# A decoder layer in split precision: three of four output pieces split by adding transfers, output pieces first in a block

## The chip, the cores and the metric

The kernel runs on one core of one Trainium2 chip. The core has a matrix engine (TensorE, here PE, whose weight loads the profile lists as PEld), a vector engine (VectorE, DVE), an activation engine (ScalarE, ACT), a general engine (GpSimd, POOL) and a queue engine (SyncE, SP). Transfers are issued from the queues of SP, ACT and POOL and carried by 16 DMA engines. SBUF is the on-chip memory, PSUM the small memory into which PE accumulates. The metric is device time in microseconds (us), lower is better.

## The reference

One decoder layer on 256 tokens of width 2048, in float32: a half-step SwiGLU FFN, layer norm, a mixer with sparse attention and a gated recurrence, layer norm, a second half-step FFN, layer norm. The change touches only the two FFNs. Of the reference, cut:

```
def swiglu(h, w_in, w_out):
    a, b = jnp.split(h @ w_in, 2, axis=-1)
    return (jax.nn.silu(a) * b) @ w_out
...
    h = layer_norm(DN_ALPHA * h + 0.5 * swiglu(h, ffn1_w_in[l], ffn1_w_out[l]), ln1_g[l], ln1_b[l])
    ... # mixer
    h = layer_norm(DN_ALPHA * h + 0.5 * swiglu(h, ffn2_w_in[l], ffn2_w_out[l]), ln3_g[l], ln3_b[l])
```

The inner width is 5632, so `w_in` is 2048 x 11264 and `w_out` 5632 x 2048.

## The kernel before

**Split precision.** PE multiplies in a format (fp32r) narrower than float32. Every operand is split into a high part (rounded by an ACT copy) and a low part (what is left), and a product is three matmuls: high x high, high x low, low x high (lines 743 to 745). The weights are used once each, so all of them have to be split while the kernel runs. That is the work of class `Weights`.

**Pieces.** All weights, in the order of their use, form one list of pieces. PE takes them one by one (`unit`, L282). A piece is one of these:

- An *output piece* ("o" in a plan): 128 x 1024 of `w_out`, 12 matmuls of 512 columns. It is loaded into a `raw` tile (4 buffers).
- A *form*: the `w_in` weights of a block come as four chunks, 1 MB each, in `rf` tiles (two buffers and a third that is used every third time). A chunk is multiplied by a scheme with seven products in place of eight, in four forms that need sums of sub-blocks: `p1q3` (12 matmuls of 256 columns; its sum `ws`, L230), `p2` (6; its sum is written at L234), `q5p7` (12; L237 writes a sum that q4p6 will need, and q5p7 reads `ws`), `q4p6` (12).

**Two ways to split.** The usual way (`split_to`, L246): ACT copies the piece to the high part of an `hl` tile (L275), DVE subtracts to get the low part (L276). There are five `hl` buffers. The other way, for pieces in the list `far` (`far_to`, L167): ACT writes minus the rounded value into two half-width tiles `wd` (L182), a POOL transfer then *adds* the weights from memory into them (L183), which leaves the low part, and ACT copies the high part into two more `wd` tiles (L185). Such a piece uses ACT and the transfers and no DVE. Its four `wd` tiles come from the pool of 128 x 512 tiles with tag `u`, which has 53 buffers and also holds the activations (`xs` or `hs`, 16 tiles), their sums for the forms (`sh`, `sl`, 16 tiles) and the gated activations `g`.

**The order.** The instructions of PE, SP and POOL run in program order; those of ACT and DVE are ordered by the framework's scheduler. When PE comes to piece `cur`, `unit` first splits far pieces up to `cur + 12` (EARLY) and loads far pieces up to 4 (LOADS) beyond those, then loads other pieces up to `cur + 8`, splits them up to `cur + 4` (AHEAD), and then takes one step of the background tasks.

**Blocks and segments.** An FFN has 22 blocks of 256 inner columns, in segments (`SEGS`) of 2 and then five times 4 blocks. For each block PE computes the products of `w_in`; DVE and ACT apply the gate (`gate`, tile `z`, L1132 to L1145). Some pieces into the next block PE transposes the result (L1151), and ACT and DVE split it into two `g` tiles (L878, L879). How many pieces after the block this happens is LAG_T, (7, 6): 7, and 6 for the last block. A segment of four blocks makes eight `g` tiles. They are multiplied by `w_out` during the *next* segment: each of its four blocks takes one quarter nb of the output columns, in four output pieces k = 0, 2, 4, 6, piece k using `g[k]` and `g[k+1]`. The product is then copied (`yd`, L1174) and added to memory by a POOL transfer (L1175).

The plan of a block says where its output pieces stand among its 16 forms. In blocks 6 to 21 three stand at the front and one behind the eighth form (`block_plan` with `lead` 3). Far pieces are those with k = 2 and 6; in the first segment's outputs, which have k = 0 and 2 only, k = 2 of the last two quarters.

Of the kernel before, what the change touches and what calls it, by code (L numbers as in the profile page):

```python
# [22 lines left out]
SEGS = ((0, 2), (2, 6), (6, 10), (10, 14), (14, 18), (18, 22))  # L23
# [39 lines left out]
AHEAD = 4  # L63
EARLY = 12
LOADS = 4
FORMS = ("p1q3", "p2", "q5p7", "q4p6")
PIECE = 1024
FAST = (0, 1, 2, 3)
# [4 lines left out]
def block_plan(chunks, fills, lead=2, n=4, late=True):  # L73

    plain = [("c", k) for q in range(n) if q not in chunks for k in (4 * q, 4 * q + 2)]
    forms = [(f, q) for q in chunks for f in FORMS]
    rest = ["o"] * fills
    plan = [(rest.pop(), 0) for _ in range(min(lead, fills))] + plain[:1]  # L80
    plain = plain[1:]
    slow = []
    while plain or rest:
        for which in (plain, rest) if late else (rest, plain):
            if which:
                p = which.pop(0)
                slow.append((p, 0) if p == "o" else p)
    if not forms:
        return plan + slow
    step = len(forms) / (len(slow) + 1)  # L90
    n = 0
    for i, f in enumerate(forms):
        plan.append(f)
        while len(slow) > n and i + 1 >= (n + 1) * step:
            plan.append(slow[n])
            n += 1
    return plan


FOUR = tuple(range(6, 22))  # L100


def layer_plans():
    three = (1, 2, 3)
    plans = [block_plan((), 0)] * 2
    plans += [block_plan((1, 3), 2, 0)] + [block_plan(three, 2, 2, late=False)] * 3
    for n in range(6, NBK):
        plans.append(block_plan(FAST if n in FOUR else three, 4, 3))
    return plans


FILLS = [(g, nb, 2 * p) for g, (b0, b1) in enumerate(SEGS[:-1]) for nb in range(4) for p in range(b1 - b0)]
PLANS = layer_plans()
FAST_MORE = (2, 3, 1)
AWAY = (0, 1, 4, 7, 10, 13)
# [13 lines left out]
OUT_LAST = ([(nb, k) for nb in (0, 1) for k in (0, 2, 4)] + [(nb, 6) for nb in (0, 1)]  # L129
            + [(nb, k) for nb in (2, 3) for k in (0, 2, 4, 6)])  # L130

LAG_T = (7, 6)
LAG_LN = 4
WIDE = 2
LAG_ROPE = 6
# [2 lines left out]
class Weights:  # L138
# [28 lines left out]
    def far_to(self, i):  # L167


        nc = self.nc  # L170
        while self.far_loaded < len(self.far) and self.far[self.far_loaded] <= i + LOADS:
            k = self.far[self.far_loaded]
            ap = self.pieces[k][0]
            t = self.far_raw[k] = self.pool.tile([P, PIECE], F32, name=f"raw{k}", tag="raw", bufs=RAW_BUFS)
            nc.sync.dma_start(t, ap)
            self.far_loaded += 1
        while self.far_split < len(self.far) and self.far[self.far_split] <= i:
            k = self.far[self.far_split]
            ap, t = self.pieces[k][0], self.far_raw.pop(k)
            h, l = ([self.wide() for _ in range(2)] for _ in range(2))  # L180
            for c in range(2):
                nc.scalar.activation(l[c], t[:, c * 512:(c + 1) * 512], AF.Copy, scale=-1.0)  # L182
                nc.gpsimd.dma_start(l[c], ap[:, c * 512:(c + 1) * 512], accum_op=OP.add)  # L183
            for c in range(2):
                nc.scalar.activation(h[c], t[:, c * 512:(c + 1) * 512], AF.Copy)  # L185
            self.hl[k] = (h, l)
            self.far_split += 1
# [58 lines left out]
    def split_to(self, i, step=PIECE):  # L246
        nc = self.nc
        while self.split <= min(i, len(self.pieces) - 1):
# [28 lines left out]
            self.hl[self.split] = (h, l)  # L277
            if form in (None, FORMS[-1]):
                del self.raw[k]
            self.split += 1  # L280

    def unit(self, n):  # L282
        if self.cur < 0 or self.off == self.size(self.cur):
# [3 lines left out]
            self.far_to(self.cur + EARLY)  # L287
            self.load_to(self.cur + AHEAD + LOADS)
            self.split_to(self.limit or min(self.cur + AHEAD, self.cap))
# [78 lines left out]
def tile_layer(ctx, tc, x_fm, x_tm, pos, f1a, f1o, wA, wki, wB, wG, lru, wab, wrb, wo, f2a, f2o,  # L368
# [41 lines left out]
    def plain(aps):  # L410
        for ap in aps:
            for o in range(0, ap.shape[1], PIECE):
                pieces.append((ap[:, o:min(ap.shape[1], o + PIECE)], None))

    def block_pieces(ap, plan, fills=None, fo=None):
        chunk = {}
        for f, k in plan:
            if f == "c":
                pieces.append((ap[:, k * 512:k * 512 + PIECE], None))
            elif f == "o" and not fo:  # L420
                plain([next(fills)])
            elif f == "o":
                g, nb, k = next(fills)
                if k in (2, 6) and (g or nb >= 2):
                    far.append(len(pieces))
                k += 2 * SEGS[g][0]
                pieces.append((fo[nb][:, k * 512:k * 512 + PIECE], None))
            else:
                if k not in chunk:
                    chunk[k] = ap[:, k * 2048:(k + 1) * 2048]  # L430
                pieces.append((chunk[k], f))

    def ffn_pieces(fa, fo):
        fills = iter(FILLS)
        for n, plan in enumerate(PLANS):
            block_pieces(fa[n], plan, fills, fo)
        for nb, k in OUT_LAST:
            k += 2 * SEGS[-1][0]
            plain([fo[nb][:, k * 512:k * 512 + PIECE]])
# [5 lines left out]
    for i, b in enumerate(A_ORDER):  # L445
        if b is None:
            plain([wki])
        elif i == 0:
            plain([wA[b]])
        else:  # L450
            block_pieces(wA[b], PLANS_A[i], early)
    for b in range(6):
        block_pieces(wG[b], block_plan(GATE_FAST[b], 0, 0))
# [8 lines left out]
    for i in range(NR + LAG):  # L462
# [4 lines left out]
        if i >= LAG:  # L467
            g, c = divmod(i - LAG, TPG)
# [655 lines left out]
    def ffn(x, forms, ln):  # L1124
        def gate(c, e, g, i, lag, plain):

            z = W.fast_pool.tile([P, 4 * S], F32, name=name("z"), tag="z", bufs=Z_BUFS)
            z4 = z.rearrange("p (j c) -> p j c", j=4)
            a, b = z4[:, 0:4:2], z4[:, 1:4:2]
            if e:  # L1130
                p1, p6, p7, q5 = e[0][:, :S], e[0][:, S:], e[1][:, :S], e[1][:, S:]
                A.activation(z4[:, 0], p1, AF.Copy)  # L1132
                V.tensor_tensor(z4[:, 1], z4[:, 0], p6, op=OP.add)
                V.tensor_tensor(z4[:, 2], z4[:, 1], p7, op=OP.add)
                V.tensor_tensor(b, q5[:, None, :].to_broadcast([P, 2, S]), z4[:, 1:3], op=OP.subtract)
                for t in range(2):
                    w = 512 if plain or t == 0 else S
                    zt = z[:, t * 512:t * 512 + w]
                    V.tensor_tensor(zt, zt, c[t][:, :w], op=OP.add)  # L1139
                A.activation(a, a, AF.Silu)  # L1140
            else:
                for t in range(2):
                    A.activation(z4[:, 2 * t], c[t][:, :S], AF.Silu)
                    A.activation(z4[:, 2 * t + 1], c[t][:, S:], AF.Copy)
            V.tensor_tensor(a, a, b, op=OP.mult)  # L1145
            for _ in range(lag):
                yield
            ps = BP()
            for k in range(2):
                for t in range(2):  # L1150
                    T.transpose(ps[:, k * S + t * P:k * S + (t + 1) * P], z[:, t * 512 + k * P:t * 512 + (k + 1) * P], ident)  # L1151
            with tc.high_priority() if lag == LAG_T[1] else nullcontext():
                for k in range(2):
                    hl = UHL("g")
                    split(hl, ps[:, k * S:(k + 1) * S])
                    g[i + k] = hl
# [20 lines left out]
        for s, (b0, b1) in enumerate(SEGS):  # L1177
            for n in range(b0, b1):
                c, e = blockF(x, forms, PLANS[n], fill)
                task = gate(c, e, g[s], 2 * (n - b0), LAG_T[n == NBK - 1], ("c", 0) in PLANS[n])  # L1180
                with tc.high_priority():
# [268 lines left out]
    def product(x, forms, fast):  # L1450

        c, e = blockF(x, forms, block_plan(fast, 0, 0, len(x) // 4), None)
        return (joined(c, e), True) if e else (c, False)
# [9 lines left out]
    def fetch(src):  # L1463
        r = []
        for t in range(2):
            u = U("gf")
            G.dma_start(u, src[t])
            r.append(u)
        return r
# [10 lines left out]
    for nb in range(4):  # L1480
        g, got = got, fetch(ga[nb + 1]) if nb < 3 else None
        s, _ = product(ya, ya_forms, YA_FAST[nb])
# [43 lines left out]
    for j in range(-1, NR + LAG):  # L1526
# [15 lines left out]
        if j >= LAG:  # L1542
            i = j - LAG
            g, c = divmod(i, TPG)
# [48 lines left out]
    for nb in range(4):  # L1593
        if nb == 2:
            bg.add("main", residual(ln1_g, ln1_b, away))
        s, _ = product(yrs, yr_forms, YR_FAST[nb])
        g, a = got
# [98 lines left out]
```

## Time and profile before

| | us |
|---|---|
| median of 3 runs | 2341.34 (2337.8 to 2342.86) |
| the profiled execution | 2340.27 |
| its span, first to last instruction | 2338.4 |
| first FFN, blocks 6 to 21 | 502.31 |
| second FFN, blocks 6 to 21 | 502.11 |

The page of the profile gives the busy time of each engine as a share of the span. The table of windows gives the same for a stretch of the span, in the order PE, PEld, DVE, ACT, POOL, with the granted TensorE clock (1.00 is full), the mean busy share of the 16 DMA engines and the bandwidth. In a timeline each line has the start in us from the span's start, the duration in us, engine, line of the kernel, operation, the tile written and those read, and shapes. The duration of an instruction includes some overlap with the next one, so costs are read from start to start. "x2" marks two like instructions in a row. A bracket gives the idle time before an instruction and what ended it. In the list of waits stand the total in us, the number of waits, and the longest.

### The profile page before, as it was taken

Reading aid. Unit: us, or ns where it says so; the run is one execution under the profiler, and the core shown is the slowest. Engines: PE = TensorE matmul, PEld = TensorE weight load, DVE = VectorE, ACT = ScalarE, POOL = GpSimd, SP = SyncE. Lnnn points to the kernel's source line nnn. Section 1 sums busy time; section 2 is a strip of 40 time slices with the busy share of each in tenths; the row PEclk is TensorE's granted clock in tenths of the full one; section 3 lists DMA queues with packets and bytes.
Section 4 is the critical chain, followed back from the end, with each engine's and each line's share of the span. In section 5 each row is a group of like instructions: output and inputs, shape, how many; then the busy total and the mean of one; then the engine's idle time right before and its main releaser. Section 6 shows DMA issues by size and latency. Waiting matters only on the chain.

```text
span 2338.4 us, 40427 instructions
## 1 busy us (share of the span) xinstructions
PE 2312.5 (99%) x15430; PEld 2109.4 (90%) x15430; DVE 2201.5 (94%) x3196; ACT 1560.0 (67%) x2273; POOL 263.4 (11%) x368
## 2 busy tenths in 40 slices
PE   9999999999999999999999999999999999999998
PEld 7899999999988999888899998888889999999997
DVE  7999999999999999979887888998999999999997
ACT  7667777777757656556557785555667777777763
POOL 1101111111110000000100001100111111111111
PEclk9999999999999999999999999999999999999999
DMA  9878988888876556554675658655788888888875
GB/s 336 251 238 240 261 250 251 250 256 250 230 244 209 192 187 216 185 189 154 244 239 193 200 182 326 239 198 195 242 275 232 253 255 252 243 252 267 244 221 215
DMA packets 142178, 546.97 MB, mean 234 GB/s; under 512 B 16640, under 2 KB 17280, under 8 KB 117536
## 3 DMA queue, kind: packets, MB, share of 16 engines
q1 hardware_dynamic: 100800, 455.00, 55.1%
q0 software_dynamic: 41040, 89.27, 18.4%
q8 instruction: 120, 1.97, 0.3%
q14 instruction: 74, 0.61, 0.1%
q10 hardware_dynamic: 144, 0.13, 0.0%
HBM read 507.10 MB, written 37.22 MB: 233 GB/s over the span
## 4 chain that ended last, share of the span: by engine, by line
PE 66%; DVE 23%; issue 5%; DMA 3%; ACT 2%; POOL 0%; SPq 0%; ACTq 0%; DVEq 0%; POOLq 0%
PE mm L743 13%; PE mm L745 13%; PE mm L744 13%; DVE hl L276 13%; PE bp L744 5%; PE bp L745 5%; PE bp L743 4%; PE mm L1390 3%; PE mm L1389 3%; PE mm L1391 3%; DVE ws L230 2%; DVE rf L237 2%; DVE rf L234 2%; ACT hl L275 2%; DMA raw<-f1o 1%
## 5 line engine op out<-in xcount | busy, mean ns | idle before, releaser
L275 ACT ACTIVATE hl<-rf 128x1024 fp32r<-128x1024 f32 x573 | 511.3, 912 | 232.9 <-DVE rf L237 119.7
L276 DVE TENSOR_TENSOR hl<-rf,hl 128x1024 fp32r<-128x1024 f32 x573 | 596.9, 1047 | 8.2 <-ACT hl L275 3.8
L276 DVE TENSOR_TENSOR hl<-raw,hl 128x1024 fp32r<-128x1024 f32 (+3 forms) x402 | 474.2, 1196 | 62.2 <-ACT hl L275 61.4
L275 ACT ACTIVATE hl<-raw 128x1024 fp32r<-128x1024 f32 (+3 forms) x402 | 408.4, 1035 | 179.4 <-PE mm L745 82.8
L744 PE MATMUL bp<-hl,sh 128*128 128x256 f32 x1146 | 323.6, 282 | 10.1 <-DVE hl L276 10.1
L743 PE MATMUL bp<-hl,sh 128*128 128x256 f32 x1146 | 320.9, 280 | 0.0
L745 PE MATMUL bp<-hl,sl 128*128 128x256 f32 x1146 | 320.2, 279 | 0.0
L743 PE MATMUL mm<-hl,hs 128*128 128x512 f32 (+1 forms) x800 | 274.5, 343 | 1.6 <-DVE z L1139 0.7
L275 ACT ACTIVATE hl<-ws 128x1024 fp32r<-128x1024 f32 x191 | 202.0, 1058 | 102.7 <-DVE ws L230 71.5
L744 PE MATMUL mm<-hl,hs 128*128 128x512 f32 (+1 forms) x800 | 268.3, 335 | 0.0
L745 PE MATMUL mm<-hl,hs 128*128 128x512 f32 (+1 forms) x800 | 267.9, 335 | 0.1
L230 DVE TENSOR_TENSOR ws<-rf 128x1024 f32<-128x1024 f32 x191 | 233.8, 1224 | 5.4 <-DMA rf<-wrb 1.3
L276 DVE TENSOR_TENSOR hl<-ws,hl 128x1024 fp32r<-128x1024 f32 x191 | 234.2, 1226 | 1.8 <-ACT hl L275 1.7
L744 PEld LDWEIGHTS bp<-hl,sh 128*128 128x128 f32 x1146 | 215.4, 188 | 17.5 <-DVE hl L276 16.3
L745 PEld LDWEIGHTS bp<-hl,sl 128*128 128x128 f32 x1146 | 217.7, 190 | 0.0
L743 PEld LDWEIGHTS bp<-hl,sh 128*128 128x128 f32 x1146 | 215.4, 188 | 1.3
L1389 PE MATMUL mm<-hs,hl 128*128 128x256 f32 x640 | 178.3, 279 | 0.0
L1391 PE MATMUL mm<-hs,hl 128*128 128x256 f32 x640 | 177.8, 278 | 0.0
L1390 PE MATMUL mm<-hs,hl 128*128 128x256 f32 x640 | 177.7, 278 | 0.0
L743 PEld LDWEIGHTS mm<-hl,hs 128*128 128x128 f32 x800 | 150.4, 188 | 19.1 <-issue 2.6
L745 PEld LDWEIGHTS mm<-hl,hs 128*128 128x128 f32 x800 | 151.0, 189 | 16.7 <-DVE hs L937 0.5
L744 PEld LDWEIGHTS mm<-hl,hs 128*128 128x128 f32 x800 | 150.5, 188 | 14.3 <-DVE hl L276 0.2
(360 smaller groups left out, 5897.6 us busy)
## 6 DMA issues: line engine op xcount, KB each, us to landing
rf<-f1a SPq DMA_DIRECT2D x75, 1024.0 KB, 7.7
rf<-f2a SPq DMA_DIRECT2D x75, 1024.0 KB, 7.5
raw<-f1o SPq DMA_DIRECT2D x88, 512.0 KB, 6.6
raw<-f2o SPq DMA_DIRECT2D x88, 512.0 KB, 6.6
raw<-wB SPq DMA_DIRECT2D x80, 512.0 KB, 4.8
raw<-wG SPq DMA_DIRECT2D x54, 512.0 KB, 4.2
ya<-yd POOLq DMA_DIRECT2D x80, 256.0 KB, 7.4
rf<-wA SPq DMA_DIRECT2D x20, 1024.0 KB, 5.5
```

Source lines behind the costliest of these rows:

```text
L230: v.tensor_tensor(t, b[:, 0:4:3], b[:, 1:2].to_broadcast([P, 2, 2, 256]), op=OP.add)
L234: v.tensor_tensor(b[:, 1], t[:, 1], b[:, 0], op=OP.add)
L237: v.tensor_tensor(b[:, 0], b[:, 1], b[:, 2], op=OP.add)
L275: nc.scalar.activation(hp, src, AF.Copy)
L276: self.last = nc.vector.tensor_tensor(lp, src, hp, op=OP.subtract)
L743: T.matmul(ps, xh, w[0], start=start, stop=False)
L744: T.matmul(ps, xh, w[1], start=False, stop=False)
L745: T.matmul(ps, xl, w[0], start=False, stop=stop)
L1389: T.matmul(ps[:, :S], w[0], x[:, 0], start=first, stop=False)
L1390: T.matmul(ps[:, :S], w[0], x[:, 1], start=False, stop=False)
L1391: T.matmul(ps[:, :S], w[1], x[:, 0], start=False, stop=last)
```

## The change

- In blocks 7 to 21 other than the first of a segment (6, 10, 14 and 18), all four output pieces stand in front of the forms. In the first blocks of a segment the plan stays at three and one.
- Far pieces are now k = 2, 4 and 6, so in blocks 6 to 21 three of four output pieces are split by ACT and adding transfers. That is 16 pieces more in each FFN: 32 ACT copies become 128 (of half the width), 32 DVE subtractions fall away, 64 POOL transfers of 256 KB are added.
- Far pieces are loaded up to eight pieces ahead of their ACT copies, before four.
- LAG_T is (5, 6): the transposes of a block's result come two pieces earlier.

```
+FAR_LOADS = 8
...
-        plans.append(block_plan(FAST if n in FOUR else three, 4, 3))
+        plans.append(block_plan(FAST if n in FOUR else three, 4, 3 if any(n == b for b, _ in SEGS) else 4))
...
-LAG_T = (7, 6)
+LAG_T = (5, 6)
...
-        while self.far_loaded < len(self.far) and self.far[self.far_loaded] <= i + LOADS:
+        while self.far_loaded < len(self.far) and self.far[self.far_loaded] <= i + FAR_LOADS:
...
-                if k in (2, 6) and (g or nb >= 2):
+                if k in (2, 4, 6) and (g or nb >= 2):
```

## The prediction

> **What bounds the kernel now.** I read the busy times first, then a table of windows cut at the starts of blocks, then the waits of PE, then the timelines of PE, DVE and ACT inside one block, and the transfers last.
>
> ```profile
> span 2338.4 us, 40427 instructions
> PE 2312.5 (99%) x15430; PEld 2109.4 (90%) x15430; DVE 2201.5 (94%) x3196; ACT 1560.0 (67%) x2273; POOL 263.4 (11%) x368
> ```
> ```profile
> core 0: us, PE busy (x) PEld busy (x) DVE busy (x) ACT busy (x) POOL busy (x), PEclk, DMA share, GB/s
> 159.30:190.20 30.90, 30.90 (x222) 29.02 (x221) 30.75 (x38) 22.93 (x32) 5.33 (x6) 1.00 0.76 224
> 598.68:630.08 31.40, 31.12 (x223) 29.02 (x221) 31.29 (x39) 22.80 (x33) 5.30 (x6) 1.00 0.84 249
> 1843.72:1875.12 31.40, 31.01 (x223) 28.91 (x222) 31.29 (x39) 22.79 (x34) 5.30 (x6) 1.00 0.89 258
> ...
> 159.30:661.61 502.31, 497.64 (x3522) 464.44 (x3521) 500.04 (x608) 361.08 (x504) 85.97 (x100) 1.00 0.85 247
> ...
> 1781.32:2283.43 502.11, 497.32 (x3522) 463.81 (x3521) 500.37 (x609) 360.57 (x503) 85.72 (x100) 1.00 0.83 247
> ```
>
> Blocks 6 to 21 of the two FFNs are 502.31 and 502.11 us, 43% of the span, and the change lives there. One block takes 502.31 / 16 = 31.39 us. In it DVE is busy 31.29 of 31.40: DVE sets the period, PE follows. Block 6 (159.30) shows what PE needs when DVE is not late: 30.90.
>
> ```profile
> PE bp L744 <- DVE hl L276: 10.1, 30, 0.6
> ```
> ```profile
> 595.41 0.28 PE L743 MATMUL bp<-hl,sh 128*128 128x256 f32 x1
> 595.96 0.38 PE L744 MATMUL bp<-hl,sh 128*128 128x256 f32 x1 [0.28 <-DVE hl L276]
> ...
> 598.68 0.39 PE L743 MATMUL mm<-hl,g 128*128 128x512 f32 x1
> ...
> 606.63 0.39 PE L745 MATMUL mm<-hl,g 128*128 128x512 f32 x1
> 606.85 0.28 PE L743 MATMUL bp<-hl,xs 128*128 128x256 f32 x1
> ...
> 610.27 0.28 PE L745 MATMUL bp<-hl,sl 128*128 128x256 f32 x1
> 610.39 0.60 PE L1151 MATMUL bp<-ident,z 128*128 128x128 f32 x4
> 610.74 0.37 PE L743 MATMUL mm<-hl,xs 128*128 128x256 f32 x1
> ...
> 611.52 0.28 PE L743 MATMUL bp<-hl,sh 128*128 128x256 f32 x1
> ...
> 616.85 0.28 PE L745 MATMUL bp<-hl,sl 128*128 128x256 f32 x1
> ```
>
> Four things are to be seen. PE waits about once in a block, here 0.55 us from 595.41 to the next start (a step is 0.12), in form q5p7 of the last chunk. An output piece is 12 matmuls of 512 columns, and the step is (606.63 - 598.68) / 35 = 0.2271. The forms before the transposes step by (610.27 - 606.85) / 29 = 0.1179, those after them by (616.85 - 611.52) / 47 = 0.1134: behind a run of 512-column matmuls PE takes 0.0045 more for each 256-column one, until the transposes (or sometimes a wait) end it. The transposes take 0.35.
>
> ```profile
> 561.48 0.69 DVE L234 TENSOR_TENSOR rf<-ws,rf 128x512 f32<-128x512 f32 x1
> 562.08 0.68 DVE L276 TENSOR_TENSOR hl<-rf,hl 128x512 fp32r<-128x512 f32 x1
> ...
> 565.72 2.36 DVE L276 TENSOR_TENSOR hl<-raw,hl 128x1024 fp32r<-128x1024 f32 x2
> 567.99 1.22 DVE L230 TENSOR_TENSOR ws<-rf 128x1024 f32<-128x1024 f32 x1
> 569.12 0.41 DVE L1133 TENSOR_TENSOR z<-z,bp 128x256 f32<-128x256 f32 x1
> 569.45 1.22 DVE L276 TENSOR_TENSOR hl<-rf,hl 128x1024 fp32r<-128x1024 f32 x1
> ...
> 606.79 0.69 DVE L1145 TENSOR_TENSOR z<-z 128x512 f32<-128x512 f32 x1
> ```
>
> On DVE a 1024-wide operation costs 1.14 from start to start ((567.99 - 565.72) / 2), a 512-wide one 0.60 (562.08 - 561.48), one of 256 from PSUM 0.33 (569.45 - 569.12). One chunk, its four forms, is four wide and three narrow ones (L230 and L276 of p1q3, q5p7, q4p6; L234, L237 and L276 of p2): 6.36.
>
> **The change, part by part.** *Far k=4.* Of the four output pieces of a block three, not two, are split without DVE: 32 more in both FFNs. DVE loses one L276 of 1.14: 31.29 - 1.14 = 30.15 per block. ACT swaps one full copy for four half copies:
>
> ```profile
> 614.96 1.14 ACT L182 ACTIVATE wd<-raw 128x512 fp32r<-128x512 f32 x2
> 616.01 1.14 ACT L185 ACTIVATE wd<-raw 128x512 fp32r<-128x512 f32 x2
> 617.05 0.62 ACT L275 ACTIVATE hl<-rf 128x512 fp32r<-128x512 f32 x1
> 617.57 1.05 ACT L275 ACTIVATE hl<-ws 128x1024 fp32r<-128x1024 f32 x1
> 618.52 1.14 ACT L182 ACTIVATE wd<-raw 128x512 fp32r<-128x512 f32 x2
> ```
>
> Four halves are 2.09 (614.96 to 617.05), the full copy 0.95: ACT goes from 22.8 to 23.9 of some 31, cost nothing. POOL issues two more additions per block.
>
> ```profile
> L183 POOL DMA_DIRECT2D wd<-f1o x68: 862/1226/1945, 88.2 to 624.3; - x68
> L183 POOL DMA_DIRECT2D wd<-f2o x68: 862/1227/1938, 1709.9 to 2244.9; - x68
> ...
> DMA to landing us min/median/max: 5.9/9.5/16.1
> ```
>
> At 1.2 each POOL goes from 5.3 to 7.8. The order of its queue is written by hand, so the six additions stand behind the block's two `yd` transfers, which follow the fourth piece by two ACT half copies (10.9 + 1.0, some +12 us from the block's start), and are issued by about +19; with the longest landing shown, 16.1, the last is there at +35, while PE wants it at 31.2 + 8.2 = +39. Cover 4 us: nothing, and us for us beyond that.
>
> *Four pieces first* (12 of 16 blocks). PE then runs 48 x 0.2271 = 10.90, transposes 0.35 with 0.10 lost just after them (610.74 to 611.52 is 0.78 for six steps), and 168 x 0.1134 = 19.05, all forms at the fast step: 30.4 if nothing is late. But the weights for forms go through five `hl` buffers. While PE works on output pieces DVE can fill five forms (chunk 0 and one of chunk 1) and then has no buffer until PE finishes the first form, at 11.35 + 12 x 0.1134 = 12.71. The ACT copy into it takes 0.52, so DVE resumes at 13.23 with p2 (0.60), q5p7 and q4p6 of chunk 1 (2.28, their sums done earlier), chunk 2 (6.36) and chunk 3 up to q5p7 (5.22): done at 27.69. PE wants that operand at 11.35 + (3 x 42 + 18) x 0.1134 = 27.68. With the q5p7 copy (0.95) outlasting the 0.60 on DVE, and some more such steps, I take a wait of 0.8, where PE waits now: 31.2 per block. Bounds: 30.4 (no wait, PE alone); and 31.9, if the two `g` splits, 0.33 each, are placed behind the freed buffer and not in the gap.
>
> *Three first* (blocks 6, 10, 14, 18). DVE's 30.15 is under PE's 30.90, and the transposes come 18 matmuls earlier: 30.90 - 18 x 0.0045 = 30.82.
>
> *Transposes earlier.* They need `z`, which DVE leaves at 606.79 + 0.69 = 607.48, +8.8 from the block's start at 598.68. They stand at +10.9 with four pieces, at 3 x 2.72 + 1.41 = +9.6 with three. Margins 2.1 and 0.8: nothing; beyond that us for us. In blocks 2 to 5 the same shift is worth 18 x 0.0045 at most in each: 0.3 in all, left out.
>
> *Loads eight ahead.*
>
> ```profile
> rf<-f1a SPq DMA_DIRECT2D x75, 1024.0 KB, 7.7
> ```
>
> They move past one `rf` load in SP's order. Four `raw` buffers take three far loads and one plain; a load that waits for its buffer holds the `rf` load behind it, which takes 7.7 to land and is wanted about two chunks of DVE, 12.7 us, later. I cost it at nothing, and the cover is 5 us.
>
> *The shared tiles.* A far piece holds four of 53 `u` tiles from its copies to its matmuls. In the third block of a segment (8, 12, 16, 20) I count from the code 16 of x, 16 of its form operands, 8 `g` of the segment being multiplied out and 4 of the new: 44. Before, 8 more fitted. Now the next block wants 12: 56, three too many. In order of issue those are the second low half and both high halves of the next block's k=6. The next tile free is `g[0]`, after the first half of that block's first piece: +1.36. The copy takes 0.6, and then the addition must land. With the median: 1.4 + 0.1 + 0.6 + 9.5 = 11.6. PE needs that half at 3 x 2.72 + 1.36 + 0.23 = 9.75. Wait 1.9, say 2.0 with the semaphores; 0 at the shortest landing, 8.4 at the longest. Four blocks per FFN.
>
> The Trainium skill (DMA: Bandwidth & Descriptors, Anatomy of one DMA) fits a GpSimd-issued transfer with 2.0 us + bytes / 436e3, an estimate of 2.6 us for these 256 KB. By that the late half would be there at +4.7, without any wait, and the sum below would be that of rival 1. No landing in the trace is under 5.9, so I go by the trace.
>
> Sum for one FFN: 4 x 30.82 + 12 x 31.2 = 497.7, against 502.2 now: -4.5. Shared tiles: 4 x 2.0 = +8.0. Net +3.5, twice +7. The profiled execution took 2340.27 (span 2338.4 and 1.9 around it), 1.1 under the median 2341.34: 2340.3 + 7 = 2347, and 2348 beside the median. A measurement tells about 0.2%, 4.7 us, from no change.
>
> **The rivals.** *1. No shortage of tiles, or its half lands in time* (tiles are handed out in another order, so that a `g` copy waits in place of the half). For it: output pieces free tiles just when the copies want them, 2 of 12 per 1.36 us. Against: the `g` copies come earlier in program order. Then only -4.5 twice: 2341.3 - 9 = 2332. The Trainium skill's fit above would give this one.
>
> *2. Everything hides.* DVE's freed 1.14 reaches PE whole: 12 x 30.4 + 4 x 30.82 = 488.1, -14.1 twice: 2313. For it: PE's own need is that. Against: the five buffers, which hold only 6.1 us of PE's work.
>
> *3. The transfers become the bound.*
>
> ```profile
> q0 software_dynamic: 3480, 6.34, 29.7%
> ```
>
> That row is for four blocks (315 to 441 us): 24 additions took 0.297 x 126 = 37.4 us of all 16 engines, 1.56 each. Two more per block bring 0.84 x 31.4 + 3.1 = 29.5 of 31.2, a share of 0.94; the highest that a block above shows is 0.89. If 0.89 were a ceiling the block would take 29.5 / 0.89 = 33.1, +1.7 in 32 blocks: 2341 + 54 = 2395. It decides from where an `rf` load takes over 12.7 us to land. Against: in DVE's list of waits this is the only one for the first FFN's `rf` loads.
>
> ```profile
> DVE ws L230 <- DMA rf<-f1a: 0.4, 1, 0.4
> ```
>
> *4. The long wait.* As forecast, but the half lands at 12 us or is copied late: wait 4.5, 8 x 4.5 - 9 = +27: 2368.
>
> **How the numbers follow.** Forecast (wait 1.2 to 3.5 each, 2341 to 2360): 0.42. Rival 1: 0.25. Rival 2: 0.10. Rival 4: 0.16. Rival 3: 0.07. Slower by over 0.2% are most of the forecast (0.27), rivals 3 and 4: 0.50. The same: 0.14 of the forecast and 0.06 of rival 1, 0.20. Faster: the rest of rival 1, rival 2, 0.01 of the forecast: 0.30. The range leaves out rival 2, the far end of rival 4 and rival 3: 2325 to 2369; the forecast's own is 2341 to 2360.
>
> **What would show it.** Right: blocks of 31 to 31.4 with four pieces and 30.8 with three; DVE busy 30.2 in each; PE's wait in q5p7 of the last chunk still there, and DVE idle about 1 us after the output pieces; in blocks 9, 13, 17 and 21 of each FFN a PE wait for a `wd` addition in the fourth output piece, its ACT copy after the block's start. Wrong: no such wait (rival 1), no wait at all (2), DVE waiting for `rf` (3). What would upset the sum most is how early the copies are handed their tiles.

## The result, and the profile after

| | before | after |
|---|---|---|
| median, us | 2342.1 (4 runs, 2337.8 to 2342.95) | 2371.34 (4 runs, 2370.58 to 2373.64) |
| ratio, 95% interval | | 1.0131 [1.0115, 1.0147] |
| span of the profiled execution | 2338.4 | 2369.1 |
| blocks 6 to 21, first and second FFN | 502.31, 502.11 | 516.02, 515.88 |

The changed kernel is 29 us slower; the forecast was 7 slower, and the range ended 2.3 us below the result. The blocks 6 to 21 account for 13.7 + 13.8 = 27.5 of it. Lines of the changed kernel are those of the kernel before plus one.

The page:

```profile
span 2369.1 us, 40549 instructions
PE 2321.6 (98%) x15430; PEld 2108.3 (89%) x15430; DVE 2177.3 (92%) x3164; ACT 1593.5 (67%) x2369; POOL 317.5 (13%) x432
```

The windows, cut at the starts of four successive blocks (10 to 13) and at the ends of the stretch:

```profile
288.39:320.26 31.87, 31.48 (x223) 29.03 (x222) 30.44 (x38) 23.76 (x35) 7.02 (x8) 1.00 0.86 238
320.26:352.89 32.63, 31.40 (x223) 29.26 (x221) 30.84 (x38) 23.25 (x34) 7.01 (x8) 1.00 0.97 277
352.89:385.56 32.67, 31.30 (x223) 28.77 (x222) 30.47 (x38) 22.99 (x33) 6.13 (x7) 1.00 0.90 263
385.56:417.79 32.23, 31.51 (x223) 29.18 (x221) 30.50 (x38) 25.57 (x38) 7.90 (x9) 1.00 0.91 263
...
159.82:675.84 516.02, 501.92 (x3522) 464.40 (x3521) 488.22 (x592) 375.97 (x548) 111.28 (x130) 1.00 0.90 260
1798.28:2314.16 515.88, 501.71 (x3522) 464.13 (x3521) 488.23 (x592) 375.74 (x548) 111.23 (x130) 1.00 0.90 260
```

Neither PE nor DVE fills a block any more. Before, DVE was busy 500.04 of 502.31. Now it is busy 488.22, which is 0.74 less in each block, but the stretch is 516.02: DVE idles (516.02 - 488.22) / 16 = 1.74 us in each block, where it idled 0.14. The freed time came back as idle time, and more with it. The block with three pieces first (288.39) is the shortest of the four.

The list of waits shows for whom:

```profile
PE mm L745 <- DVE hl L277: 19.5, 27, 1.2
PE bp L745 <- DVE hl L277: 11.0, 30, 0.6
...
DVE hl L277 <- ACT hl L276: 104.0, 162, 2.4
...
DVE g L880 <- ACT g L879: 10.3, 27, 0.5
...
ACT wd L186 <- PE mm L745: 21.1, 16, 2.3
```

PE waits for DVE as before, only longer. DVE waits for ACT's copies. No wait of PE for a `wd` addition is there, so the wait on which the forecast laid 16 us did not come. And ACT, busy in only two thirds of the time, is late. Its timeline in the block from 320.26 says why:

```profile
330.67 1.28 ACT L1175 ACTIVATE yd<-mm 128x512 f32<-128x512 f32 x2 [2.46 <-PE mm L746]
331.85 0.38 ACT L879 ACTIVATE g<-bp 128x256 fp32r<-128x256 f32 x1
332.72 0.38 ACT L879 ACTIVATE g<-bp 128x256 fp32r<-128x256 f32 x1 [0.49 <-DVE g L880]
333.00 0.62 ACT L183 ACTIVATE wd<-raw 128x512 fp32r<-128x512 f32 x1
333.52 0.62 ACT L276 ACTIVATE hl<-rf 128x512 fp32r<-128x512 f32 x1
...
338.97 1.14 ACT L183 ACTIVATE wd<-raw 128x512 fp32r<-128x512 f32 x2
340.01 1.14 ACT L186 ACTIVATE wd<-raw 128x512 fp32r<-128x512 f32 x2
341.06 1.04 ACT L276 ACTIVATE hl<-ws 128x1024 fp32r<-128x1024 f32 x1
342.00 1.14 ACT L183 ACTIVATE wd<-raw 128x512 fp32r<-128x512 f32 x2
343.05 0.61 ACT L186 ACTIVATE wd<-raw 128x512 fp32r<-128x512 f32 x1
343.57 2.51 ACT L276 ACTIVATE hl<-rf 128x1024 fp32r<-128x1024 f32 x3
```

and DVE's beside it:

```profile
332.26 0.42 DVE L880 TENSOR_TENSOR g<-bp,g 128x256 fp32r<-128x256 f32 x1 [0.35 <-ACT g L879]
...
334.17 0.69 DVE L277 TENSOR_TENSOR hl<-rf,hl 128x512 fp32r<-128x512 f32 x1 [0.56 <-ACT hl L276]
335.12 1.22 DVE L277 TENSOR_TENSOR hl<-ws,hl 128x1024 fp32r<-128x1024 f32 x1 [0.26 <-ACT hl L276]
...
342.13 1.22 DVE L277 TENSOR_TENSOR hl<-ws,hl 128x1024 fp32r<-128x1024 f32 x1 [0.45 <-ACT hl L276]
...
345.26 2.95 DVE L277 TENSOR_TENSOR hl<-rf,hl 128x1024 fp32r<-128x1024 f32 x3
```

Two things are to be seen. Just behind the output pieces (which end at 331.16) DVE loses 0.35 + 0.56 + 0.26 = 1.17: all five `hl` buffers are full, and the first copy into a freed one comes at 333.52, behind two `g` copies and a `wd` copy. Later four, then three `wd` copies stand in a row ahead of a form's copy. PE pays for that at the end of chunk 2:

```profile
331.71 0.28 PE L745 MATMUL bp<-hl,xs 128*128 128x256 f32 x1
...
344.90 0.28 PE L746 MATMUL bp<-hl,sl 128*128 128x256 f32 x1
...
346.53 0.39 PE L745 MATMUL mm<-hl,xs 128*128 128x256 f32 x1 [1.23 <-DVE hl L277]
```

PE steps by (344.90 - 331.71) / 112 = 0.1178 here, though the transposes are behind it: this is the slow step, where the forecast had 0.1134.

From this there were two theories. **Theory A, ACT's queue:** the twelve copies of a block's three far pieces fall due at three successive pieces of PE, form bunches in ACT's order, and hold the forms' copies. **Theory B, the buffers:** behind four output pieces in a row five `hl` buffers can't carry DVE, whatever ACT does.

### The profile page after: what moved, and what is told of

It is laid out like the page before. It is cut to its first block, busy times and chain, and to the rows that moved or that the text cites. A ratio compares the mean times of both kernels' runs of the same rounds, so it can differ in the third digit from the quotient of the medians.

```text
span 2369.1 us, 40549 instructions
## 1 busy us (share of the span) xinstructions
PE 2321.6 (98%) x15430; PEld 2108.3 (89%) x15430; DVE 2177.3 (92%) x3164; ACT 1593.5 (67%) x2369; POOL 317.5 (13%) x432
## 4 chain that ended last, share of the span: by engine, by line
PE 77%; DVE 13%; ACT 6%; issue 3%; DMA 2%; POOL 0%; SPq 0%; ACTq 0%; DVEq 0%; POOLq 0%
PE mm L745 16%; PE mm L746 16%; PE mm L744 16%; DVE hl L277 7%; PE bp L745 5%; PE bp L746 5%; PE bp L744 5%; PE mm L1392 3%; PE mm L1390 3%; PE mm L1391 3%; ACT hl L276 2%; DVE ws L231 2%; ACT wd L186 1%; ACT wd L183 1%; DVE rf L235 1%
## 5 line engine op out<-in xcount | busy, mean ns | idle before, releaser
L276 ACT ACTIVATE hl<-rf 128x1024 fp32r<-128x1024 f32 x573 | 505.9, 909 | 192.9 <-PE mm L746 91.3
L276 ACT ACTIVATE hl<-raw 128x1024 fp32r<-128x1024 f32 (+3 forms) x370 | 377.9, 1033 | 175.3 <-PE mm L746 89.8
L277 DVE TENSOR_TENSOR hl<-raw,hl 128x1024 fp32r<-128x1024 f32 (+3 forms) x370 | 436.1, 1190 | 57.2 <-ACT hl L276 56.0
L277 DVE TENSOR_TENSOR hl<-ws,hl 128x1024 fp32r<-128x1024 f32 x191 | 232.8, 1219 | 30.6 <-ACT hl L276 30.5
L276 ACT ACTIVATE hl<-ws 128x1024 fp32r<-128x1024 f32 x191 | 201.5, 1055 | 59.4 <-DVE ws L231 23.9
```

Of the source, the lines that this page charges most:

```text
L276: nc.scalar.activation(hp, src, AF.Copy)
L277: self.last = nc.vector.tensor_tensor(lp, src, hp, op=OP.subtract)
```

## The experiments

All ratios are to the kernel before, on the same chip. "Spread" means that the far copies are issued one at a time:

```
+            self.far_parts += [(k, 1, 0), (k, 1, 1), (k, 0, 0), (k, 0, 1)]
...
+        n = 1
+        while self.far_parts and (n > 0 or min(self.far_parts)[0] <= self.cur + 2):
+            n -= 1
+            part = next((x for x in self.far_parts if x[1]), self.far_parts[0])
```

(each part is one copy, the low ones with their addition). In kernels with this edit the lines are 12 further than in the kernel before.

| run | pieces first | far | copies | transposes (LAG_T) | median us | ratio [95%] |
|---|---|---|---|---|---|---|
| before | 3 | k=2,6 | bunched | 7 | 2340 to 2342 | 1 |
| after | 4 | k=2,4,6 | bunched | 5 | 2371.34 | 1.0131 [1.0115, 1.0147] |
| e1_spread | 4 | k=2,4,6 | spread | 5 | 2363.05 | 1.0098 [1.0083, 1.0113] |
| e2_order | 4 | k=2,6 | bunched | 5 | 2362.74 | 1.0098 [1.0081, 1.0114] |
| e3_far | 3 | k=2,4,6 | bunched | 7 | 2347.52 | 1.0032 [1.0020, 1.0044] |
| e4_far_spread | 3 | k=2,4,6 | spread | 7 | 2329.84 | 0.9956 [0.9941, 0.9971] |
| e5_lag | 3 | k=2,4,6 | spread | 5 | 2324.03 | 0.9927 [0.9912, 0.9941] |
| e13_three | 3 | k=2,4,6 | bunched | 5 | 2327.63 | 0.9939 [0.9923, 0.9956] |

### The changed kernel with spread copies (e1_spread)

> The changed kernel, but the twelve ACT copies of a block's three far pieces are issued one at a time, one for each piece that PE begins (low halves first), and no longer four at a time at three pieces in a row. Order of pieces, number of instructions, buffers and loads stay. Theory A (ACT's queue): in the changed kernel DVE idles 1.73 us a block because far copies stand ahead of form copies in ACT's order; spread, the idle at +21.9 (0.45) and at +14.9 (0.26) of a block with four pieces first goes, and so does most of the 1.3 in a block with three: 24 x 0.7 + 8 x 1.3 = 27, so 2344 (2335 to 2352). Theory B (five hl buffers behind four output pieces hold DVE, whatever ACT copies between): no change, 2371 within 4.

Measured: 2363.05, 8 less, and neither theory's number. The windows of one ordinary block and the list of waits:

```profile
355.22:387.05 31.83, 30.98 (x223) 28.64 (x221) 30.53 (x38) 22.86 (x33) 6.97 (x8) 1.00 0.91 265
```
```profile
PE mm L756 <- DMA wd<-f1o: 4.7, 4, 2.2
PE mm L756 <- DMA wd<-f2o: 2.9, 4, 1.0
```

Blocks with four first fall from 32.2 to 32.7 (after) to 31.8, those with three from 31.85 to 31.3: the bunches cost 0.4 to 0.9 a block, as theory A has it. But the second block of a segment got longer (33.19 at 322.03; 36.97 at worst, where the granted clock is 0.93 for the first 17 us), since the copies now come so late that PE waits for eight additions. And an ordinary block still takes 1.0 more than with three first (below). That rest is left for theory B; the run with six buffers below splits it.

### The order alone (e2_order)

> The kernel before with the order alone: four pieces first and transposes two units earlier, far pieces still k=2 and k=6, loads four ahead. Theory A: DVE keeps 31.3 of work a block, adds the idle behind the freed buffer (0.35 + 0.56) but has four far copies fewer in its way: some 32.2 in the 24 blocks with four first, 2341 + 24 x 0.8 = 2361 (2352 to 2368). Theory B: DVE's 31.3 plus the whole idle of 1.6: 32.9 in 24 blocks, 2341 + 36 = 2377.

The edit is the `block_plan` line and LAG_T of the diff, nothing else. Measured: 2362.74, at theory A's number, but the block is not wholly A's:

```profile
319.30:351.34 32.04, 31.47 (x222) 29.13 (x221) 31.57 (x39) 22.94 (x33) 5.26 (x6) 1.00 0.84 253
```
```profile
ACT wd L182 <- DMA raw<-f1o: 6.2, 3, 2.2
...
ACT wd L182 <- DMA raw<-f2o: 4.7, 3, 1.7
```

DVE's 31.57 and 0.47 of idle time make 32.04, near the expected 32.2. In the fourth block of a segment, 33.3 on the mean in the first FFN, ACT waits for a far load: with four pieces first, loads four ahead come too late. That is some 8 us of the total, which theory A did not have, so that its number was met in part by luck. The order by itself costs 22.6 us, and the longer lead of the loads belongs to it.

### The far pieces alone, bunched and spread (e3_far, e4_far_spread)

```
+FAR_LOADS = 8
...
-                if k in (2, 6) and (g or nb >= 2):
+                if k in (2, 4, 6) and (g or nb >= 2):
```

with `FAR_LOADS` in place of `LOADS` in `far_to`; the second run adds the spreading.

> The kernel before with the far pieces alone: k=4 is far too and loads begin eight ahead; three pieces first and the transposes as before. Theory A: DVE has 30.5 of work a block and idles 0.5 to 0.7 behind bunches of eight far copies: 31.1 a block, 2341 - 32 x 0.3 = 2332 (2325 to 2341). Theory B: without four pieces first DVE does not idle, PE alone sets 30.9: 2341 - 16 = 2325 (2321 to 2328).

> The run with the far pieces alone (three pieces first), with its far copies issued one at a time as in the first run of this group. Theory A: the idle behind bunches goes, PE sets the block at 30.9: 2325 (2320 to 2330), some 7 under the run without the spreading. Theory B: the same time as without the spreading, 2325.

Measured: 2347.52 bunched (its profiled execution took 2352.09), slower than before and than both theories; 2329.84 spread. The same instructions in another order are worth 17.7 us. Of the 21 us between the two profiled executions, 11.6 lie in blocks 6 to 21 of the two FFNs and most of the rest ahead of them. In the bunched kernel, ACT and DVE in the block from 259.53, one of six that take some 32:

```profile
278.06 1.14 ACT L183 ACTIVATE wd<-raw 128x512 fp32r<-128x512 f32 x2
279.10 1.14 ACT L186 ACTIVATE wd<-raw 128x512 fp32r<-128x512 f32 x2
280.14 1.04 ACT L276 ACTIVATE hl<-ws 128x1024 fp32r<-128x1024 f32 x1
```
```profile
278.86 0.69 DVE L238 TENSOR_TENSOR rf<-rf 128x512 f32<-128x512 f32 x1
281.22 1.22 DVE L277 TENSOR_TENSOR hl<-ws,hl 128x1024 fp32r<-128x1024 f32 x1 [1.67 <-ACT hl L276]
```

Four `wd` copies, 2.08 us, stand ahead of one form's copy, and DVE idles 1.67 for it. Spread, one of the blocks reads:

```profile
255.82:286.72 30.90, 30.90 (x222) 29.01 (x221) 30.44 (x38) 24.55 (x37) 7.86 (x9) 1.00 0.93 274
```

PE is busy in all of it, and nearly all 32 blocks take 30.90. Theory A is shown for this place. The bunched kernel was worse than A's number because the idle (0.4 to 1.7) varies from block to block, and because its block 6 begins at 166.12 and not at 159.30, with a like loss ahead of the second FFN's; in the spread one it is 163.12.

### Block 6 without the third far piece (e6_nb3)

e4_far_spread with

```
+                if k in (2, 4, 6) and (g or nb >= (3 if k == 4 else 2)):
```

> The run with three pieces first, far k=4 and spread copies, but in block 6 (the first with far pieces) k=4 is not far. With it block 6 begins 3.8 us later than in the kernel before (163.12 against 159.30), and ACT waits 6.3 us for far loads ahead of it. If the third far load among the plain pieces of blocks 4 and 5 is the cause (four raw buffers): 3.8 in each FFN comes back, 2329.8 - 7.6 = 2322. If loads eight ahead as such are (with two far pieces as well): no change, 2330.

Measured: 2329.27, ratio 0.9950 [0.9935, 0.9965]. Block 6 began at 160.64, but the median hardly moved: the expectation's case of no change. What the early blocks lose is not settled by it, since loads only four ahead changed nothing in e5_lag either (e11_loads4).

### The transposes alone (e5_lag)

The edit to e4_far_spread is `LAG_T = (5, 6)`.

> The run with three pieces first, far k=4 and spread copies (2329.8), with the transposes two units earlier as in the changed kernel. It asks which half of the order costs: four pieces first or the earlier transposes. If the earlier transposes cost nothing: 18 matmuls a block at 0.1134 and not 0.1179, 30.82 a block, 2329.8 - 3 = 2327. If they are the cost of the order (their splits of g then fall where DVE and ACT are short): up to the 0.9 a block of the order, 2329.8 + 29 = 2359.

Measured: 2324.03, 5.8 under e4_far_spread.

```profile
252.58:283.40 30.82, 30.82 (x222) 28.94 (x221) 30.43 (x38) 25.30 (x38) 7.92 (x9) 1.00 0.94 265
160.07:653.24 493.17, 493.17 (x3522) 462.99 (x3521) 486.32 (x593) 376.73 (x550) 111.80 (x131) 1.00 0.94 271
```

A block takes 30.82, which is the prediction's number for three pieces first to the last digit. Earlier transposes are a gain; four pieces first are the harm in the order.

### The changed kernel with three pieces first (e13_three)

> The changed kernel with one thing undone: three pieces first in every block; its far copies stay four at a time, loads eight ahead, transposes two units earlier. It asks how the two costs add. If they are separate (far copies in bunches 2347.5 - 2329.8 = 17.7 with three pieces first): 2324.0 + 17.7 = 2342, 29 under the changed kernel. If four pieces first are what makes bunches harmful: 2324 to 2330. If three pieces first give little back: over 2360.

The edit undoes one line of the change: `block_plan(FAST if n in FOUR else three, 4, 3)`. Measured: 2327.63, which is 43.7 under the changed kernel and 13.8 under the kernel before.

```profile
253.43:284.25 30.82, 30.82 (x223) 28.94 (x221) 29.50 (x37) 24.47 (x37) 7.94 (x9) 1.00 0.96 267
160.95:654.22 493.27, 493.27 (x3523) 463.00 (x3522) 483.91 (x593) 376.51 (x549) 111.76 (x130) 1.00 0.94 270
```

The two costs do not add. DVE still idles, 30.82 - 29.50 = 1.32 in this block and (493.27 - 483.91) / 16 = 0.58 on the mean, but here that is slack: PE is busy in all of the stretch and never waits for it. The intervals of this run and of e5_lag overlap. So bunches cost time with late transposes (17.7 us, e3_far against e4_far_spread) and behind four output pieces (8 us, the changed kernel against e1_spread), and little or nothing here. Bunched, the earlier transposes alone are worth 19.9 us (e3_far to this run). Why late ones leave no slack was not tried.

### Six buffers, and the control (e9_hl6, e10_u49)

The edit to e1_spread is `HL_BUFS = 6` and `U_BUFS = 49` in the first, `U_BUFS = 49` alone in the second.

> The changed kernel with spread copies (2363.1), with six hl buffers in place of five; the space comes from u tiles, 49 in place of 53. Theory B (five buffers fill while PE works on four output pieces, DVE pauses 1.0 to 1.2 and PE waits for that behind chunk 2): the sixth buffer lets DVE do one more form in that time, the pause goes, 24 x 0.9 = 22 less: 2341 (2335 to 2350), blocks near 30.9. Theory A (only the order of ACT's and DVE's instructions): 2363. If 49 tiles are too few, the waits for late additions at the first block behind one with three pieces grow beside it.

> The control for the run with six hl buffers: the changed kernel with spread copies, five hl buffers, 49 u tiles. It tells what the four tiles cost by themselves. If tiles aren't short: 2363 within 4. If they are (56 were counted as wanted in the third block of a segment): over 2368.

Six buffers with all 53 tiles (e7_hl6) do not fit into SBUF, so the sixth is paid for with four tiles, and the control has the four tiles fewer alone. Measured: 2375.65, ratio 1.0156 [1.0141, 1.0171], with six buffers; 2369.26, 1.0125 [1.0109, 1.0142], in the control. The first misses as a total. The control falls in its second case: 49 tiles are too few for this kernel.

```profile
PE mm L755 <- ACT wd L197: 13.6, 24, 0.7
```

In the control PE waits 24 times for a far high half; with six buffers that wait is 26.9 us long. But it falls in the third and fourth block of a segment. The second block is free of it in both, and there the two kernels differ by the buffer alone. The control, then six buffers:

```profile
318.83:350.67 31.84, 31.23 (x222) 29.11 (x221) 30.14 (x38) 22.82 (x33) 6.97 (x8) 1.00 1.01 281
```
```profile
319.63:350.85 31.22, 31.22 (x222) 29.16 (x221) 29.36 (x37) 21.88 (x32) 7.03 (x8) 1.00 1.03 284
```

Over all eight such blocks the means are 31.88 and 31.27. The sixth buffer takes 0.6 off the block and nearly all of PE's waits: theory B is shown for this part. What is left, 31.2, is PE by itself, without a wait:

```profile
331.08 0.28 PE L756 MATMUL bp<-hl,xs 128*128 128x256 f32 x1
...
347.92 0.28 PE L755 MATMUL bp<-hl,sh 128*128 128x256 f32 x1
```

143 steps in 16.84 us are 0.1178 each, and 10.90 + 0.45 + 168 x 0.1178 = 31.1. So in these blocks four pieces first do not gain even with buffers enough: three first take 30.82. No block with four first, in any run, took less than 31.18.

### Transposes still earlier (e8_lag4, e12_lag4)

Both with `LAG_T = (4, 6)`, the first from e1_spread, the second from e5_lag.

> The changed kernel with spread copies, its transposes one unit earlier still: ahead of the fourth output piece in place of behind it, so that the g splits of ACT and DVE fall into the time in which all hl buffers are full. If the g splits behind the fourth piece are what holds the first copies: idle 1.16 falls to about 0.5, 24 x 0.6 = 15 less, 2348 (2342 to 2354). If the buffers alone hold DVE: 2363 within 4. If z is not ready at +8.2 (it left DVE at +7.6 in the changed kernel), PE waits and it gets slower.

Measured: 2363.56, ratio 1.0096 [1.0079, 1.0113], no change against e1_spread. DVE's first wait (0.35, for `g`) is gone, the wait at the freed buffer is 0.7 to 0.8 and not 0.56, and the ordinary block takes 31.8 as before. Where the transposes stand relative to the fourth piece does not matter to the time: DVE still has to wait for the first free buffer.

> The fastest so far (2324.0) with the transposes one unit earlier still, directly behind the third piece at +8.2. z leaves DVE at +8.26 there, so PE waits about 0.1 and gains 12 matmuls x 0.0045 = 0.05: 2324 within 3. If z becomes later too, slower by up to 32 x 0.5 = 16.

Measured: 2346.97, ratio 1.0030 [1.0019, 1.0041]: 23 slower than e5_lag, beyond the worst that was expected.

```profile
291.74 0.66 PE L1163 MATMUL bp<-ident,z 128*128 128x128 f32 x4 [0.41 <-DVE z L1157]
```

`z` is ready at 291.00 + 0.68 - 283.00 = +8.7 here, not at +8.26: it got later together with the transposes. The last matmul of the output pieces starts at 290.94, so the transposes start 0.80 behind it, where a step is 0.23: that 0.57 is the whole of what the block (31.40) has over 30.82. Blocks 6 to 21 of the two FFNs lose 17 us, most of it in this way. Most of the rest lies between the two stretches, where DVE waits 4.6 us for one `rf` load.

### Loads four ahead (e11_loads4)

> The fastest so far (three pieces first, far k=4, spread copies, transposes two units earlier: 2324.0) with far loads four ahead as in the kernel before, in place of eight. If the longer lead of the loads is needed with three far pieces: ACT waits for raw loads ahead of form copies, slower, 2330 or more. If it only costs (raw buffers held longer among the plain pieces of blocks 4 and 5): 2322 or less. If it does nothing: 2324 within 3.

The edit to e5_lag is `FAR_LOADS = 4`. Measured: 2323.77, ratio 0.9931 [0.9916, 0.9946], the same as with eight. This and e5_lag are the fastest versions, 0.7% under the kernel before.

## Why the prediction was wrong

**Four pieces first is the step that failed.** Put at 31.2 a block; the mean of the 24 blocks is 32.43. That is 24 x 1.23 = +30. It was mis-sized in two places, and its lower bound in a third.

- *The pause behind the output pieces, and DVE's own work.* The mechanism was right: five buffers fill, DVE idles about 1 us, PE waits for it. Its size was not. The prediction let the copy into the freed buffer start at once, and DVE resumes at +13.9, not at +13.23: the buffer comes free some 0.2 later, a `wd` copy in ACT's order holds the copy by another 0.35, and DVE follows the start of that copy by 0.65, not by 0.52. (The 0.26 before the second copy was in the prediction, as 0.95 against 0.60.) And DVE's work is 30.5 a block, not 30.15. With spread copies the pause is the same, 0.35 + 0.56 + 0.26, and the block is 31.8: 30.53 of work and 1.30 idle, nearly all of it this pause. That is 0.6 above the forecast.
- *"ACT goes from 22.8 to 23.9 of some 31, cost nothing."* A mean load says nothing about a queue worked in order. The twelve copies fall due at three successive pieces, and DVE waits behind them: 31.8 to 32.4, another 0.6.
- *PE's own need.* The prediction had all 168 steps at 0.1134 behind the transposes. They can stay at 0.1178 nearly throughout, as in the block with six buffers, which alone brings PE to 31.1. This adds nothing to the 1.23: in the spread run the block from 355.22, mostly fast steps, and the one from 387.05, mostly slow ones, both take 31.8, because DVE sets them. But it is a floor, and the bound of 30.4 was not reached by any run.

**Three pieces first** was put at 30.82. Without four first in the neighbouring blocks it is 30.82 in e5_lag and e13_three. In the changed kernel it is 31.69 on the mean, 8 x 0.87 = +7. Far copies for the next block, twelve in a bunch, fall into this one; spread, it is 31.20 (e1_spread), so that the bunch explains about half. The other half stays open.

**The shared tiles** were put at +16, by a wait of PE for a late addition in blocks 9, 13, 17 and 21. It did not come; rival 1 was right on this. The shortage itself is there: ACT waits for a tile once in the third block of each segment (2.1 to 2.3 us) and twice in the fourth (0.5 each), 25.1 us in all, 21.1 of it in the row above. But it is the copy of a high half (L186), which needs no transfer after it, and PE comes to it later: no wait for a `wd` tile stands in its list. With 49 tiles the same wait does reach PE. That tiles run short was right; the half that waits was wrong.

By the prediction's own terms: +7, less 16, plus 30, plus 7, is 28; the blocks lost 27.5. The two errors had opposite signs, so the forecast was nearer than its parts deserved.

**What held.** DVE's saving is there, but smaller: 500.04 - 488.22 is 0.74 a block as busy time, not 1.14. An operation that stands alone counts 1.22 and one in a row 1.14, and in blocks 6 to 21 of the first FFN 104 operations now end before the next one begins, where 35 did. With three pieces first, earlier transposes cost nothing and gave 18 x 0.0045 a block (e4_far_spread to e5_lag: 30.90 to 30.82, some 2.6 of the 5.8 us; the rest came ahead of block 6, which began at 160.07 and not at 163.12). Loads eight ahead cost nothing (e11_loads4). Rival 3 fell: blocks with a DMA share of 0.94 and 0.96 take 30.82, so 0.89 was no ceiling. Rival 2's number, 2313, needs 30.4 in every block with four first, and none came under 31.18; the nearest to it is 2324, with the order that the change gave up. Rival 4's time, 2368, was close, by a mechanism that did not occur.

The weighing of the landing time ended like this:

```profile
wd<-f1o POOLq DMA_DIRECT2D x100, 256.0 KB, 7.5
```

The Trainium skill's fit (DMA: Bandwidth & Descriptors, Anatomy of one DMA), from which an estimate of 2.6 us was worked out, is far from this median too. That it forecast "no wait" rightly is no support: the addition was not the late half.

## What to carry to other kernels

An engine with a third of its time free can still set the pace if its queue is worked in order: look at what stands directly ahead of the instruction that the bottleneck waits for, and issue side work in single steps between the urgent ones. When work is gathered at one place, ask how many buffers the engine behind it can fill meanwhile; here four output pieces in a row outlasted five buffers, and undoing that one line made a change that lost 1.3% into one that gains 0.6%. And price a change part by part on the chip, and the parts together: the far pieces alone, bunched and with late transposes, lost 0.3%, and gained with the copies spread or the transposes earlier.

## What the runs showed of the hardware

- PE's slow step for 256-column matmuls (0.1178 against 0.1134) behind a run of 512-column ones is not always ended by the transposes: it lasted through all 168 in some blocks with four pieces first, and was gone within a few steps in others (in the block from 352.89, all but some 20 are fast). In the changed kernel the transposes stand directly behind the fourth piece, and the forms behind them begin with the slow step in 16 of 24 blocks; where one or three forms stand between, they begin with the fast step in all blocks (8 of 8 there, 32 of 32 in the kernel before). A wait of PE often ends the slow step. What decides is open.
- The landing time of the adding transfers does not follow their number: the median is 9.5 us with 68 an FFN in the kernel before and 7.4 with as many in e2_order, 7.5 with 100 in the changed kernel, and 7.1 to 9.9 in the other runs with 100. What sets it was not tried.
